# First products on tokens that are not normed yet: factor and shift applied to the sums

## The chip, the cores and the metric

The kernel runs on one core of one Trainium2 chip. The metric is the device time of one execution in microseconds (us), from three runs of the kernel.

## The reference, cut to what matters

A layer of a diffusion trunk over 384 tokens (128 context tokens and 256 latent tokens), width 2048. The adaLN modulation gives a scale and a shift for each feature and kind of token; the tokens are normed, modulated and multiplied by one large projection:

```
mod = silu(c) @ w_ada + b_ada                      # six parts of 2048
h = rmsnorm(x, norm_mix) * (1.0 + sc1) + sh1       # x: 384 x 2048
z = h @ w_in                                       # w_in: 2048 x 5632, eleven groups of 512 columns
```

Four token mixers work on the groups of `z`; an output projection, a second modulated norm and a gated MLP follow (`w_out`, `w_up`, `w_down`).

## The kernel before

Features lie on the partitions. The 2048 features are 16 row tiles of 128, and a token tile `x[i]` holds four of them (128 x 4 x 384). Every float32 product is made of three matmuls on rounded halves: high by high, high by low, low by high (`mm_a`, `mm_b`). The weights come as chunks of 128 x 1024; ScalarE casts a chunk to its high half `whi`, VectorE subtracts for the low half `wlo`.

The projection `w_in` runs in three rounds over the row tiles: tiles 0 and 1, tiles 2 to 5, tiles 6 to 15 (`ROUNDS`). In each round all eleven groups (V, GBV, U, DX, CC, CH, CB and four heads H0 to H3) take their part, and their sums are kept in SBUF as `z`, first copied by ScalarE (`ev_first`), then added by VectorE (`ev_add`). Between the chunks of a round stand chunks of `w_ada`, so that scale and shift of the next row tiles are there in time. Most of these are matmuls of few columns on PE (`ada_pe`); the tile `START_DVE` is summed by VectorE (`ada_dve`, the tile `aacc`) and brought into columns by matmuls (`ps_mod`, L502).

At the start, `input_squares`, `input_pairs`, `input_sums` and `input_norm` compute the norm of all tokens: ScalarE squares, VectorE adds pairs, PE sums over the partitions (`ps_n`, L428), ScalarE takes the root, VectorE the reciprocal `bc1`. Then `split_affine` makes row tile 0: times `bc1` on VectorE, scale and shift on ScalarE, cast to `hh`, low half `hl`. The first chunks (`win_duo`) hold two groups of one row tile each: V with GBV, U with DX. `keep_warm` issues matmuls whose result nobody reads.

The order of the instructions on every engine is written by a planner (`Pipe`), which books an estimated cost for each instruction on a clock per engine. DMAs are issued on SP's queue in the order of the chunks; chunks marked `early` come first. Work outside the main stream (low halves, norms, evacuations that are more than one instruction) runs in threads; a thread that doesn't split weights is held back while the booked backlog of VectorE or ScalarE is over 2.5 us. All large tiles come from one pool of 20 slots.

The helpers for VectorE and ScalarE record every operation under L90, so the profile tells them apart by their tiles.

Of the kernel before, what the change touches and what calls it, by code (L numbers as in the profile page):

```python
# [14 lines left out]
P = 128  # L15
D = 2048
# [20 lines left out]

ROUNDS = ((0, 2), (2, 6), (6, 16))
# [8 lines left out]
WARM = (6, 8)  # L47
# [9 lines left out]
T_DMA = 1.46  # L57
TABLES = (AF.Silu, AF.Sigmoid, AF.Gelu_apprx_tanh, AF.Exp, AF.Sqrt)
# [35 lines left out]
class Pipe:  # L94
# [5 lines left out]
    def __init__(self, nc, pools, look_dma, look_split, backlog):  # L100
        self.nc = nc
        self.V = Engine(nc.vector, self, "d", 0.075, 1.04e-3, 0.52e-3, ("tensor_copy", "tensor_scalar"))
        self.S = Engine(nc.scalar, self, "a", 0.1, 0.83e-3, 0.83e-3, ())
        self.pools = pools
        self.LD, self.LS = look_dma, look_split
        self.backlog = backlog
        self.chunks = []
        self.threads = []
        self.now = 0.0
        self.clock = {"d": 0.0, "a": 0.0, "q": 12.0}  # L110
        self.end = 0.0
# [44 lines left out]
    hold = True  # L156
# [38 lines left out]
    def run(self):  # L195
        n = len(self.chunks)
        nxt, ahead, loaded = 0, 0, 0
        for c in sorted((c for c in self.chunks if "early" in c), key=lambda c: c["early"]):
            self.dma(c)
        for i in range(-1, n):  # L200
# [4 lines left out]
            while loaded < n:  # L205
                if "early" in self.chunks[loaded] or self.chunks[loaded].get("spare") is not None:
                    loaded += 1
                    continue
# [26 lines left out]
def trunk(ctx, tc, a, o):  # L235
# [28 lines left out]
    def slot(name, dtype=F32, shape=(P, 4, T)):  # L264
        return sp.tile(list(shape), dtype, tag="s", name=name)
# [141 lines left out]
    n1 = {}  # L407

    def input_squares(i):
        add_pos(x[i], i, pos, posr)  # L410
        n1[i] = slot("sq0")
        for k in range(0, 4, 2):
            S.activation(n1[i][:, k:k + 2], x[i][:, k:k + 2], AF.Square)
# [6 lines left out]

    def input_pairs(i):
        V.tensor_add(n1[i][:, 0:2], n1[i][:, 0:2], n1[i][:, 2:4])

    def input_sums(i):
        if i == 0:
            n1["ps"] = misc("ps_n1")
        for k in range(2):
            PE.matmul(n1["ps"][:, 0:T], ones, n1[i][:, k], start=i == 0 and k == 0, stop=i == 3 and k == 1)  # L428

    def input_norm():  # L430
        v1 = row_tile("v1")
        S.activation(v1, n1["ps"][:, 0:T], AF.Sqrt, bias=eps, scale=1.0 / D)
        V.reciprocal(bc1, v1)
# [111 lines left out]

    h_done, h_queue, h_workers = set(), [], []

    def h_worker():
        while h_queue:
            yield from h_make(h_queue.pop(0))  # L550
        h_workers.pop()

    def h_make(j):
# [3 lines left out]
        if j == 0:  # L557
            yield next(parts)
            pipe.hold = False
            pipe.finish(pipe.splits[0])  # L560
# [29 lines left out]
    def win_duo(i, k):  # L590
        def mm(c):
            need_h(k + 1)
            for n, grp in enumerate(DUOS[i]):
                n_acc, width = win_shape(grp)
                if k == 0:
                    z[grp] = slot(f"z{grp}", shape=(P, n_acc, width))
                for m in range(n_acc):
                    t = acc("acc0")
                    s = slice(512 * n, 512 * n + 512)
                    yield win_product(grp, t, m, k, c["hi"][:, s], c["lo"][:, s], True, True)  # L600
                    (ev_add if k else ev_first)(z[grp], m, t[:, 0:width])
        return dict(src=a["w_in_1"][i, k], mm=mm)

    def win_group(grp, rnd, evac):
# [4 lines left out]
        for k0 in range(k_lo, k_hi, 2):  # L609
            def pre(k0=k0):  # L610
                if rnd < 2 or grp == 0:
                    need_h(k0 + 2)
                if rnd == 2 and k0 == k_lo:
# [7 lines left out]
            def mm(c, k0=k0):  # L621
                if k0 == k_lo:
                    accs.extend(acc(f"acc{m}") for m in range(n_acc))
                    if rnd == 0:
                        z[grp] = slot(f"z{grp}", shape=(P, n_acc, width))
                hi = c["hi"].rearrange("p (k n) -> p k n", k=2)
                lo = c["lo"].rearrange("p (k n) -> p k n", k=2)
                for m in range(n_acc):
                    for kk in range(2):
                        yield win_product(grp, accs[m], m, k0 + kk, hi[:, kk], lo[:, kk], k0 + kk == k_lo, k0 + kk == k_hi - 1)  # L630
                    if k0 + 2 == k_hi:
# [267 lines left out]
    def rounds(rnd, evac):  # L899
# [3 lines left out]
        out.insert(1, win_duo(0, 1))  # L903
        out.insert(3, win_duo(1, 1))
        return out

    def make_h(js):
        h_queue.extend(js)
        for _ in range(min(2 - len(h_workers), len(js))):
# [3 lines left out]
    def ada_first(j):  # L913

        place = [(0, j, 1), (1, j, 1)]
        return [dict(ada_pe(a["w_ada_0"][j, k4], (0, -j), 4 * k4, 4, place, lambda: make_h((j,))), spare=-1) for k4 in range(4)]
# [16 lines left out]
    for rnd, (k0, k1) in enumerate(ROUNDS):  # L933
        ada = [c for j2s in START[rnd] for cs in zip(*[two_by_two(j2) for j2 in j2s]) for b in cs for c in b]
        if rnd == 0:
            t0, t1, d0, d1 = ada_first(0), ada_first(1), win_duo(0, 0), win_duo(1, 0)
            for i, c in enumerate(t0 + [d0, t1[0], d1] + t1[1:]):
                c["early"] = i
            side = t0 + [d0] + t1 + [d1]
# [261 lines left out]
    for i in range(4):  # L1201
        input_squares(i)
        if i:
            input_pairs(i - 1)
            input_sums(i - 1)
    input_pairs(3)
    input_sums(3)
    input_norm()
    pipe.chunks[4]["pre"] = lambda: (keep_warm(WARM[1]), need_h(1))
# [119 lines left out]
```

## Time and profile before

| | us |
|---|---|
| runs | 1779.76, 1780.69, 1780.70 |
| median | 1780.69 |
| the profiled execution | 1778.78 |
| its span, first to last instruction | 1777.0 |

| engine | busy us | share of the span |
|---|---|---|
| PE (TensorE, matmuls) | 1743.4 | 98% |
| DVE (VectorE) | 1113.9 | 63% |
| ACT (ScalarE) | 699.9 | 39% |
| POOL (GpSimd) | 20.4 | 1% |

Matmuls are pipelined, so a busy PE need not be PE at its peak: the distance from start to start tells more. An idle engine costs nothing unless another one waits for it; the profile names for each wait what ended it.

### The profile page before, as it was taken

What the parts mean: (1) busy time and instruction counts of PE and PEld (TensorE: products, weight loads), DVE (VectorE), ACT (ScalarE), POOL (GpSimd) and SP (SyncE); (2) the same over time, 40 slices, a digit from 0 to 9 for tenths busy, and PEclk for the clock granted to TensorE, in tenths of its full rate; (3) what the DMA queues carried; (4) which work ended last, traced back from release to release, by engine and by line L of the source; (5) the groups of instructions that cost most, each with busy time, mean ns of one, the idle gap of its engine ahead of it and who ended that gap; (6) DMA issues with size and microseconds to landing.
All of it is one profiled execution on the core that took longest, in us unless ns stands there. A gap on an engine that the chain in (4) does not pass through costs nothing.

```text
span 1777.0 us, 27701 instructions
## 1 busy us (share of the span) xinstructions
PE 1743.4 (98%) x11244; PEld 1680.6 (95%) x11244; DVE 1113.9 (63%) x1911; ACT 699.9 (39%) x1044; POOL 20.4 (1%) x35
## 2 busy tenths in 40 slices
PE   8999999999999999999999999999999999999996
PEld 6989889999989989999999999999999999999996
DVE  4595678888986577899884344465453345545444
ACT  5523333234743256343342223344332234434331
POOL 0000000000001000000000000000000000000000
PEclk9999999999999999999999999999999999999998
DMA  8878776576645855656654444434444444444431
GB/s 335 285 281 307 283 250 229 182 251 213 221 132 181 289 212 158 196 184 206 210 177 136 127 123 130 128 117 135 130 121 130 130 122 129 129 124 127 131 119 72
DMA packets 89664, 317.29 MB, mean 179 GB/s; under 512 B 9856, under 2 KB 14208, under 8 KB 89536
## 3 DMA queue, kind: packets, MB, share of 16 engines
q1 hardware_dynamic: 87520, 308.58, 53.5%
q0 software_dynamic: 1728, 6.55, 1.1%
q8 instruction: 88, 1.44, 0.3%
q10 hardware_dynamic: 288, 0.39, 0.1%
q14 instruction: 40, 0.33, 0.1%
HBM read 311.82 MB, written 3.67 MB: 178 GB/s over the span
## 4 chain that ended last, share of the span: by engine, by line
issue 63%; PE 7%; DVE 1%; DMA 0%; POOL 0%; ACT 0%; POOLq 0%; DVEq 0%
PE acc L520 2%; PE acc L521 2%; PE acc L522 2%; DVE xr L90 1%; DMA xr<-in_xT 0%; PE ps_sc L286 0%; PE ps_bc L286 0%; PE ps_ada L464 0%; PE ps_o L286 0%; DVE wlo L90 0%; DVE sqacc L90 0%; POOL hg_q L381 0%; PE ps_ms L286 0%; DVE hw L90 0%; ACT kq L90 0%
## 5 line engine op out<-in xcount | busy, mean ns | idle before, releaser
L90 DVE TENSOR_TENSOR wlo<-raw,whi 128x1024 fp32r<-128x1024 f32 x384 | 469.2, 1222 | 490.8 <-ACT whi L90 488.5
L90 ACT CAST whi<-raw 128x1024 fp32r<-128x1024 f32 x384 | 402.7, 1050 | 878.2 <-PE acc L521 646.0
L520 PE MATMUL acc<-h2h,whi 128*128 128x384 f32 x1408 | 470.9, 334 | 0.2 <-ACT h2h L90 0.2
L521 PE MATMUL acc<-h2l,whi 128*128 128x384 f32 x1408 | 470.5, 334 | 0.3
L522 PE MATMUL acc<-h2h,wlo 128*128 128x384 f32 x1408 | 470.3, 334 | 0.0
L520 PEld LDWEIGHTS acc<-h2h,whi 128*128 128x128 f32 x1408 | 264.3, 188 | 1.8 <-ACT h2h L90 1.0
L521 PEld LDWEIGHTS acc<-h2l,whi 128*128 128x128 f32 x1408 | 264.3, 188 | 0.8 <-DVE h2l L90 0.8
L522 PEld LDWEIGHTS acc<-h2h,wlo 128*128 128x128 f32 x1408 | 264.3, 188 | 0.0
L522 PE MATMUL acc<-gh,wlo 128*128 128x384 f32 x704 | 235.1, 334 | 0.0
L520 PE MATMUL acc<-gh,whi 128*128 128x384 f32 x704 | 235.1, 334 | 0.0
L521 PE MATMUL acc<-gl,whi 128*128 128x384 f32 x704 | 235.1, 334 | 0.0
L520 PE MATMUL acc<-hh,whi 128*128 128x384 f32 x576 | 199.2, 346 | 0.9 <-DVE z L90 0.9
L522 PE MATMUL acc<-hh,wlo 128*128 128x384 f32 x576 | 193.3, 336 | 0.5 <-DVE wlo L90 0.4
L521 PE MATMUL acc<-hl,whi 128*128 128x384 f32 x576 | 192.8, 335 | 0.1
L90 DVE SCALAR_TENSOR_TENSOR aacc<-raw,svp,aacc 128x512 f32<-128x512 f32 x270 | 184.8, 745 | 0.0
L90 DVE SCALAR_TENSOR_TENSOR glu<-up,sm,glu 128x127 f32<-128x127 f32 (+1 forms) x352 | 135.3, 415 | 30.4 <-ACT glu L90 24.2
L520 PEld LDWEIGHTS acc<-gh,whi 128*128 128x128 f32 x704 | 132.1, 188 | 0.0
L521 PEld LDWEIGHTS acc<-gl,whi 128*128 128x128 f32 x704 | 132.1, 188 | 0.0
L522 PEld LDWEIGHTS acc<-gh,wlo 128*128 128x128 f32 x704 | 132.1, 188 | 0.0
L520 PEld LDWEIGHTS acc<-hh,whi 128*128 128x128 f32 x576 | 108.1, 188 | 11.8 <-issue 7.1
L521 PEld LDWEIGHTS acc<-hl,whi 128*128 128x128 f32 x576 | 108.2, 188 | 1.0 <-DVE hl L90 0.4
L522 PEld LDWEIGHTS acc<-hh,wlo 128*128 128x128 f32 x576 | 108.1, 188 | 1.1 <-DVE wlo L90 1.1
(154 smaller groups left out, 1540.3 us busy)
## 6 DMA issues: line engine op xcount, KB each, us to landing
raw<-in_w_up SPq DMA_DIRECT2D x176, 512.0 KB, 3.6
raw<-in_w_in SPq DMA_DIRECT2D x88, 512.0 KB, 4.7
raw<-in_w_down SPq DMA_DIRECT2D x88, 512.0 KB, 3.5
raw<-in_w_ada SPq DMA_DIRECT2D x64, 512.0 KB, 5.7
raw<-in_w_ada_dve SPq DMA_DIRECT2D x64, 512.0 KB, 4.5
raw<-in_w_ada_pe SPq DMA_DIRECT2D x64, 512.0 KB, 5.4
raw<-in_w_out SPq DMA_DIRECT2D x32, 512.0 KB, 4.3
x<-in_xT SPq DMA_DIRECT2D x4, 768.0 KB, 7.8
```

The costliest lines, as they stand in the source:

```text
L90: return f(*args, **kw)
L520: PE.matmul(out, wh, xh, start=first, stop=False)
L521: PE.matmul(out, wh, xl, start=False, stop=False)
L522: PE.matmul(out, wl, xh, start=False, stop=last)
```

## The change

Six groups of the first round (U, DX, CC, CH, CB, H0) no longer wait for the norm. Since the norm is a factor per token, `W (A x r + B) = r (W A x) + W B`: their matmuls take `uh`, `ul`, the high and low half of `A x` for tokens not yet normed, with the shift `B` as two further columns (386 columns in place of 384). When the norm is known, `fix` multiplies the kept sums by `bc1`, 24 multiplications of 128 x 384 on VectorE, and the evacuation in the second round adds the shift, per range of tokens, from the two extra columns (`ev_shift`). V, GBV and H1 to H3 work on normed tokens as before, later in the round.

So the loads of `x[1]` to `x[3]` move behind the first CC chunk, the norm becomes threads that run beside the products (squares added up by VectorE in `sqacc`, three small matmuls, a power on GpSimd, diagonal matrices, three matmuls to spread the rows), and the order of the chunks changes: U at row tile 0, the adaLN of row tile 1, DX, CC, CH, CB, H0, V with GBV twice, U with DX at row tile 1, H1 to H3. Every slot is 1568 elements long, so that all of them begin on multiples of 128 bytes though six tiles have rows of 386.

```diff
+PLAIN = (W_U, W_DX, W_CC, W_CH, W_CB, W_H0)
-WARM = (6, 8)
+WARM = (6, 3)
+AHEAD = (0.0, 3.0, 1.0)
+X_THERE = (5.0, 21.0, 23.5, 26.0)
+SLOT = 1568
...
     def run_threads(self):
         for th in list(self.threads):
             own = th[0] in self.splits
-            if own and self.hold:
-                continue
...
         for c in sorted((c for c in self.chunks if "early" in c), key=lambda c: c["early"]):
+            if c["early"] in self.between:
+                self.between[c["early"]]()
+                self.clock["q"] += 3 * T_X
             self.dma(c)
...
-    load_x(1, x[1], SY)
-    load_x(2, x[2], SY)
-    load_x(3, x[3], SY)
+    pipe.between = {len_early: lambda: [load_x(i, x[i], SY) for i in range(1, 4)] for len_early in (10,)}
...
+    def input_norm():
+        while len(squared) < 4:
+            yield 0.3
+        yield "d"
+        ps = misc("ps_n1")
+        mean_square_rows(ps, sqacc)
+        yield 0.3
+        q = rstd_of(ps, NG, D, "n1")
+        yield 0.9
+        dgs = diags(q)
+        yield
+        bc = misc("ps_bc1")
+        broadcast_rows(bc, dgs)
+        yield 0.2
+        S.copy(bc1, bc[:, 0:T])
...
+    def plain_make(j):
+        if not plain:
+            plain.extend(slot(n, F32R, (P, 2, 400)) for n in ("uh", "ul"))
+        uh, ul = plain[0][:, j, 0:T + 2], plain[1][:, j, 0:T + 2]
+        A, B, src = mods[:, 1, j], mods[:, 0, j], x[0][:, j]
+        for t0, t1, v in RANGES:
+            S.activation(uh[:, t0:t1], src[:, t0:t1], AF.Copy, scale=A[:, v:v + 1])
+        S.copy(uh[:, T:T + 2], B)
+        yield "a"
+        for t0, t1, v in RANGES:
+            V.scalar_tensor_tensor(out=ul[:, t0:t1], in0=src[:, t0:t1], scalar=A[:, v:v + 1], in1=uh[:, t0:t1].bitcast(F32), op0=ALU.mult, op1=ALU.subtract)
+        V.tensor_sub(ul[:, T:T + 2], B, uh[:, T:T + 2].bitcast(F32))
...
+    def plain_slot(grp):
+        t = slot(f"z{grp}", shape=(P, 4, T + 2))
+        return t[:, :, 0:T], t
...
+    def fix(grp):
+        i = PLAIN.index(grp)
+        while grp not in summed or i and PLAIN[i - 1] not in fixed:
+            yield 0.3
+        for m in range(4):
+            zt = z[grp][:, m]
+            V.tensor_mul(zt, zt, bc1)
+            yield 1.2
+        fixed.add(grp)
+
+    def ev_shift(grp, zt, m, t):
+        for t0, t1, v in RANGES:
+            V.scalar_tensor_tensor(out=zt[:, m, t0:t1], in0=t[:, t0:t1], scalar=wb[grp][:, m, T + v:T + v + 1], in1=zt[:, m, t0:t1], op0=ALU.add, op1=ALU.add)
...
+                if rnd == 1 and grp in PLAIN and k0 == k_lo:
+                    pipe.finish(fixes[grp])
...
+                    elif k0 + 2 == k_hi and rnd == 1 and grp in PLAIN:
+                        ev_shift(grp, z[grp], m, accs[m])
...
-        out.insert(1, win_duo(0, 1))
-        out.insert(3, win_duo(1, 1))
+        out[len(PLAIN) - 2:len(PLAIN) - 2] = [win_duo(0, 0), win_duo(0, 1), win_duo(1, 1)]
...
-            side = merge_streams(main, ada, count(ada) / (len(main) - 1.0))
+            if rnd == 1:
+                for i in range(2):
+                    main[i]["early"] = 9 + i
+            side = merge_streams(main, ada, count(ada) / (len(main) - AHEAD[rnd]))
...
-    pipe.chunks[4]["pre"] = lambda: (keep_warm(WARM[1]), need_h(1))
+    pipe.chunks[4]["pre"] = lambda: keep_warm(WARM[1])
```

## Rows read from the trace of the kernel before

**Rows 1.** The page's first part: busy us, share of the span, instructions of each engine.
```profile
PE 1743.4 (98%) x11244; PEld 1680.6 (95%) x11244; DVE 1113.9 (63%) x1911; ACT 699.9 (39%) x1044; POOL 20.4 (1%) x35
```

**Rows 2.** Windows by stage: stretch, length, busy us (instructions) per engine, granted clock, DMA.
```profile
25.98:84.60 58.62, 58.47 (x637) 52.30 (x638) 28.36 (x47) 34.86 (x64) 0.00 (x0) 1.00 0.86 304
84.60:132.00 47.40, 45.51 (x349) 39.66 (x348) 41.62 (x67) 12.69 (x16) 0.00 (x0) 1.00 0.75 266
```

**Rows 3.** Timeline of the start: start us, us, engine, line, instruction [idle before, releaser].
```profile
12.86 7.27 PE L428 MATMUL ps_n<-sq,misc_c 128*128 128x384 f32 x16 [3.01 <-DVE sq L90]
...
20.64 1.04 ACT L90 CAST whi<-raw 128x1024 fp32r<-128x1024 f32 x1
...
24.40 0.98 ACT L90 ACTIVATE ht<-ht,mods 128x128 f32<-128x128 f32 x2 [2.72 <-DVE ht L90]
...
25.98 0.50 PE L525 MATMUL acc<-whi,hh 128*128 128x512 f32 x1 [0.28 <-ACT hh L90]
```

**Rows 4.** Windows of the first 30 us; the last number is GB/s.
```profile
0.00:10.00 10.00, 5.21 (x12) 3.88 (x12) 2.22 (x7) 2.66 (x3) 0.53 (x8) 1.00 0.82 274
10.00:30.00 20.00, 16.86 (x177) 11.57 (x178) 12.31 (x23) 12.02 (x20) 0.00 (x0) 0.91 1.04 405
```

**Rows 5.** DMA issues of the first 60 us: count, size of one, median us to landing.
```profile
raw<-in_w_ada SPq DMA_DIRECT2D x23, 512.0 KB, 10.2
...
x<-in_xT SPq DMA_DIRECT2D x4, 768.0 KB, 7.8
pos<-in_pos_c ACTq DMA_DIRECT2D x1, 256.0 KB, 5.4
sm<-in_smalls SPq DMA_DIRECT2D x1, 236.0 KB, 5.5
```

**Rows 6.** PE timeline, first round: a 24-product chunk starts, an adaLN pair, the next chunk.
```profile
53.22 0.44 PE L520 MATMUL acc<-hh,whi 128*128 128x384 f32 x1
...
57.60 1.08 PE L464 MATMUL ps_ada<-raw,svp 128*32 128x128 f32 x32
58.61 0.44 PE L520 MATMUL acc<-hh,whi 128*128 128x384 f32 x1
```

**Rows 7.** PE timeline where the second round begins.
```profile
84.47 0.39 PE L525 MATMUL acc<-whi,hh 128*128 128x512 f32 x1
84.70 0.40 PE L526 MATMUL acc<-wlo,hh 128*128 128x512 f32 x1
```

**Rows 8.** Instructions on the tile `ps_bc`, a later norm's broadcast: ns min/median/max, first and last start.
```profile
L286 PE MATMUL ps_bc<-dg,misc_c x36: 271/275/579, 507.2 to 1763.5; 128*128 128x128 f32 x36
```

**Rows 9.** VectorE by line and shape, first 600 us: busy us, mean ns, idle before.
```profile
L90 DVE TENSOR_TENSOR z<-acc,z 128x384 f32<-128x384 f32 x80 | 42.0, 551 | 21.3 <-PE acc L522 21.0
...
L90 DVE TENSOR_TENSOR ht<-x,bc 128x384 f32<-128x384 f32 x16 | 8.3, 552 | 0.0
...
L90 DVE SCALAR_TENSOR_TENSOR xr<-acc,mods,xr 128x256 f32<-128x256 f32 x12 | 5.7, 475 | 0.0
...
L90 DVE SCALAR_TENSOR_TENSOR xr<-acc,mods,xr 128x128 f32<-128x128 f32 x12 | 4.2, 346 | 1.0 <-PE acc L522 0.9
```

**Rows 10.** VectorE timeline, 84.5 to 133 us: the two idle stretches in its busiest part.
```profile
104.76 1.22 DVE L90 TENSOR_TENSOR wlo<-raw,whi 128x1024 fp32r<-128x1024 f32 x1 [3.16 <-ACT whi L90]
...
114.96 1.23 DVE L90 TENSOR_TENSOR wlo<-raw,whi 128x1024 fp32r<-128x1024 f32 x1 [0.54 <-ACT whi L90]
```

**Rows 11.** PE timeline, 112 to 130 us: the three instructions that waited for VectorE.
```profile
113.54 0.44 PE L520 MATMUL acc<-hh,whi 128*128 128x384 f32 x1 [0.69 <-DVE z L90]
...
123.60 0.44 PE L520 MATMUL acc<-hh,whi 128*128 128x384 f32 x1 [0.22 <-DVE z L90]
...
128.21 1.00 PE L502 MATMUL ps_mod<-aacc,pick 128*32 128x128 f32 x16 [0.82 <-DVE aacc L90]
```

**Rows 12.** Windows around the stretch at the lower granted clock (column after POOL).
```profile
9.00:12.80 3.80, 0.85 (x3) 0.34 (x1) 2.38 (x6) 3.79 (x6) 0.00 (x0) 1.00 1.07 373
12.90:16.20 3.30, 3.30 (x5) 1.75 (x6) 3.30 (x9) 2.44 (x4) 0.00 (x0) 0.50 1.02 404
```

More of the change, by code (lines that the diff above doesn't have):

```diff
@@ L109, in __init__ @@
         self.now = 0.0
[L110 removed]
+        self.clock = {"d": 0.0, "a": 0.0, "q": T_FIRST}
         self.end = 0.0
@@ L205, in run @@
             while loaded < n:
-                if "early" in self.chunks[loaded] or self.chunks[loaded].get("spare") is not None:
+                if "early" in self.chunks[loaded] or "src" not in self.chunks[loaded] or self.chunks[loaded].get("spare") is not None:
                     loaded += 1
@@ L264, in slot @@
     def slot(name, dtype=F32, shape=(P, 4, T)):
-        return sp.tile(list(shape), dtype, tag="s", name=name)
+        t = sp.tile([P, SLOT], dtype, tag="s", name=name)
+        n = 1
+        for d in shape[1:]:
+            n *= d
+        return t[:, 0:n] if len(shape) == 2 else t[:, 0:n].rearrange("p (a b) -> p a b", b=shape[2])
     def row_tile(name):
@@ L419, in keep_warm @@
             PE.matmul(ps[:, 0:2 * P], ident, misc_c, start=True, stop=True)
[L421 to L433, printed above, removed]
     def columns(ps, n, place):
@@ L544, in h_slots, with need_plain, ev_plain @@
         hl[i] = slot(f"{name}l{i}", F32R)
+    plain, plain_done, wb = [], set(), {}
+    def plain_make(j):
[6 more added lines that the diff above has]
+        S.copy(uh[:, T:T + 2], B)
+        yield "a"
+        for t0, t1, v in RANGES:
+            V.scalar_tensor_tensor(out=ul[:, t0:t1], in0=src[:, t0:t1], scalar=A[:, v:v + 1], in1=uh[:, t0:t1].bitcast(F32), op0=ALU.mult, op1=ALU.subtract)
+        V.tensor_sub(ul[:, T:T + 2], B, uh[:, T:T + 2].bitcast(F32))
+        plain_done.add(j)
+    def need_plain(n):
+        while not all(k in plain_done for k in range(n)):
+            for th in list(pipe.threads):
+                if th in pipe.threads and th[0] not in pipe.splits + stats:
+                    pipe.step(th)
+    def plain_slot(grp):
+        t = slot(f"z{grp}", shape=(P, 4, T + 2))
+        return t[:, :, 0:T], t
+    def ev_plain(grp, zt, m, t, add):
+        if add:
+            V.tensor_add(wb[grp][:, m], t[:, 0:T + 2], wb[grp][:, m])
+        else:
+            S.copy(wb[grp][:, m], t[:, 0:T + 2])
+        if m == 3 and (add or grp not in sum(DUOS, ())):
+            summed.add(grp)
+    def fix(grp):
[10 more added lines that the diff above has]
+            V.scalar_tensor_tensor(out=zt[:, m, t0:t1], in0=t[:, t0:t1], scalar=wb[grp][:, m, T + v:T + v + 1], in1=zt[:, m, t0:t1], op0=ALU.add, op1=ALU.add)
     h_done, h_queue, h_workers = set(), [], []
@@ L549, in h_worker @@
         while h_queue:
+            while not normed:
+                yield 0.3
             yield from h_make(h_queue.pop(0))
@@ L915, in ada_first @@
         place = [(0, j, 1), (1, j, 1)]
-        return [dict(ada_pe(a["w_ada_0"][j, k4], (0, -j), 4 * k4, 4, place, lambda: make_h((j,))), spare=-1) for k4 in range(4)]
+        return [dict(ada_pe(a["w_ada_0"][j, k4], (0, -j), 4 * k4, 4, place, lambda: pipe.start(plain_make(j))), spare=-1) for k4 in range(4)]
     def ada_start(j2):
@@ L1200, in trunk @@
     keep_warm(WARM[0])
[L1201 to L1208, printed above, removed]
-    pipe.chunks[4]["pre"] = lambda: (keep_warm(WARM[1]), need_h(1))
+    add_pos(x[0], 0, pos, posr)
+    for i in range(5):
+        stats.append(input_squares(i) if i < 4 else input_norm())
+        pipe.spawn(stats[i], X_THERE[i] if i < 4 else 0.0)
+    pipe.chunks[4]["pre"] = lambda: keep_warm(WARM[1])
     pipe.run()
```

90 lines of the change are left out of this document (69 added, 21 removed).

## The prediction

> **What bounds the kernel now.** I read the page's busy table first: TensorE (PE) is busy 98% of the span [rows 1]. So a change can gain only where PE has no useful work, and lose where it makes PE wait. The windows by stage show where that is: from 25.98 to 84.60 us PE is busy 58.47 of 58.62, from 84.60 to 132 it loses 1.9 us [rows 2]. Before 25.98 it has no projection to do at all, and the timeline of the start says why [rows 3]. PE sums the squares of the four token tiles until about 20, ScalarE and VectorE turn them into the norm factor, the first normed row tile is made, and the first product of `w_in` follows at 25.98, released by that tile's cast on ScalarE (`hh`). So 26 us at the start are the prize. What limits how soon products can start without the norm is the DMA: 274 GB/s in the first 10 us, 405 from 10 to 30 [rows 4].
>
> **The change, part by part.**
>
> *The start.* A raw weight tile is 512 KB (0.524 MB), a token tile 768 KB (0.786 MB), the small tables 256 and 236 KB [rows 5], with two more of 128 x 256 and 128 x 32 numbers 0.65 MB. Two bursts matter.
>
> First product: it needs one token tile, the tables, four `w_ada_0` tiles and the pair U+DX: 0.79 + 0.65 + 5 x 0.524 = 4.06 MB. By [rows 4] 2.74 MB have moved at 10 us and the rest takes 1.32/0.405 = 3.3 us, so 13.3. From last byte to use I add 0.7, an estimate between 0 and the 1.5 us that lie between 6.42 MB (19.1 by the same sum) and the cast of the first pair at 20.64 [rows 3]. Then ScalarE casts the pair (1.04), scales the two ranges of row tile 0 (0.98 for two such ranges) and copies two columns (about 0.2): 16.2. VectorE still has the low half of the pair (1.22 [rows 10]) and that of the row tile: about 17.1. From there PE runs U (12 products, half of the 4.38 us of a 24-product chunk [rows 6]), the second `w_ada_0` tile (last byte about 19.2, done about 21), DX, and with row tile 1 (about 24) the chunk CC, done about 27.9.
>
> Second burst: CC is followed by the adaLN pair and CH. The first 13 raw tiles, four token tiles and tables are 6.82 + 3.15 + 0.65 = 10.6 MB, moved at 10 + 7.88/0.405 = 29.4; with 0.7 more the second of the pair is usable at 30.1, and CH starts at 30.9. PE waits here, so some 1.5 to 2.5 us of anything late before it cost nothing; if that cover is used up, each us late is a us lost.
>
> *From there to the end of the first round* the products are those of before: seven chunks of 24 products (CH, CB, H0, U+DX of the second row tile, H1, H2, H3) of 4.38, two of V+GBV at 18 x 0.23 + 0.2 = 4.34, seven adaLN pairs of 1.01 [rows 6, 7]: 30.7 + 8.7 + 7.1 = 46.4. Added: the norm on PE inside the stream, six matmuls for the sums, six for the broadcast, at 0.275 each [rows 8]; alone 3.2, overlapped perhaps 0.6, I take 1.3, as they sit among other matmuls. The two extra columns: 144 products x 2/384 x 0.18 = 0.1. Round two then begins at 30.9 + 46.4 + 1.4 = 78.7 instead of 84.47 [rows 7]: **5.8 us gained**. Own bounds 4.0 (norm at its full price) to 6.7. The norm's chain itself (tiles 1 to 3 landing by about 26.5, adds, power, diagonals) ends near 39; V+GBV, the first to need it, comes at about 48, so it lies beside 9 us of other work.
>
> *VectorE in the second round.* Added on it: 24 multiplications by the factor (`fix`), of the form 0.552; in the evacuation of six groups one add of 0.551 becomes two scaled adds out of PSUM, by the nearest rows 0.475 + 0.346, so +0.27 each, 24 times, or +0.19 after the 0.08 overlap of neighbours [rows 9]. Total some 11 + 5 us. Removed at the start: a reciprocal. In most of the kernel VectorE has room, but not from 88 to 132 us, where it computes an adaLN tile itself: in the VectorE timeline of that stage I find only 3.16 and 0.54 us idle [rows 10], and PE waited there for it: 0.69 and 0.22 for a group's old sums, 0.82 for the adaLN accumulators [rows 11]. Queued behind an added instruction are the low halves of weights, the evacuations and these accumulations. How many multiplications fall there is decided by the planner (threads wait while its booked backlog exceeds 2.5 us; a `fix` waits 1.2 us after each). `fix` starts when the second U chunk is summed, about 65; at one per 2 us or so eight are out before 78.7. In the stage itself the planner's own booked load fills VectorE, so I expect about one in 4 us: three or four ahead of the 3.16 idle, which hides them, three after it. Behind it: 3 x 0.47 + 8 evacuations x 0.19 = 2.9, less the 0.54 idle, = 2.4 of lag for PE to wait out. Against it, the 0.82 wait is for matmuls that the planner places by its booked clock, which now counts the added work, so they move behind PE work and that wait can vanish; part of the lag also lands after PE's last need. I take a loss of **1.0**, bounds -1.7 (all three waits gone) and 3.0.
>
> *Nothing else.* H0, CB and the rest get evacuated at the same place by the same ScalarE copy; plain casts of two row tiles cost ScalarE and VectorE some 4 us at the start, where both idle. SLOT only lays tiles out: no row shows a row start that costs, so 0; its bad case is a rival. SP's queue: the three token tiles move behind CC; everything behind them (CH, the pair) is in the second burst's sum.
>
> **Sum.** The profiled execution took 1778.78 (span 1777.0); 1778.78 - 5.8 + 1.0 = 1774.0. The median of the runs shown, 1780.69, lies 1.9 above that execution, so I forecast 1780.69 - 4.8 = **1775.9**; its own range, a gain of 7.2 to 2 (the ends of both terms hardly coincide), is 1773.5 to 1778.7.
>
> **Rivals.**
> *B, VectorE takes half of it back:* lag not absorbed, 2.5 to 5 us lost; net gain about 2, 1778.5. For it: idle of 0.54 in 27 us, and weight buffers are freed by VectorE, so lag also delays transfers. Against: the planner holds threads back when its backlog is high.
> *C, the clock:* the granted clock fell to 0.50 (1.2 GHz) in 12.9 to 16.2, after 3.8 us in which PE was busy 0.85 [rows 12]. In the changed kernel PE is busy in pieces from 10 to 17 and waits for the pair near 29. If U, the adaLN tile and DX run at half clock they take some 6 us more (2.1 + 2 + 2.1), CC ends at 34 instead of 27.9, and beyond the cover some 3.8 of the 5.8 are gone: 1779.7. The Trainium skill ("TensorE: Matmul & The Clock Gate", section on HAM oscillation) says that matmuls after a long enough wait for DMA start cold; by it this would be the forecast. The row agrees for a wait of 3 us; but over 10 to 30 us the mean granted was 0.91 [rows 4], so the level came back soon, and the waits I expect are shorter.
> *D, slower:* all 24 multiplications come ahead of the adaLN tile's last accumulation, because the planner books short. 24 x 0.47 + 12 x 0.19 = 13.6, less 3.7 idle, = 9.9 lost against 5.8: +4.1, 1784.8. It beats the gain from about 16 of them in that stretch. For it: finish() forces a group's four just ahead of its second round. Against: only U, DX and CC come due by then.
> *E, the width or the layout costs:* 144 products of 386 columns at the 0.23 of 512 columns instead of 0.18 [rows 6, 7], or rows that start off a round address: 144 x 0.05 = 7.2, so 1783.1. Nothing in the trace shows a width that falls off a step.
> *F, it doesn't do what it says:* the norm comes late and V+GBV waits for it, or row tile 0 isn't ready early. Nine us of cover speak against; it would end near 1780.
>
> **How the numbers follow.** About 0.2% (3.6 us) is what a measurement of this kernel can tell from no change. Forecast 0.60, of which 0.50 gains over 3.6 and 0.10 less; B 0.18, C 0.08 and F 0.02 all within 0.2%, less 0.03 of them faster; D 0.08 and E 0.04 slower, of which half of E stays within 0.2%. So faster 0.53, same 0.37, slower 0.10. The range leaves out D, E, and the best of the forecast: 1773.5 to 1781.0.
>
> **What would show it.** Right: the first `w_in` product at 16 to 17.5 us; CH's products at about 31, waited for by DMA; round two (the 512-column products in a row) at 78 to 79.5; multiplications in VectorE spread from 65 on, under eight between the 3.16 idle's place and the last accumulation; PE's waits for VectorE there between 0 and 4 us in sum. Wrong: PE waits between 31 and 79, a clock of 0.50 after 20 us, first products later than 20, or a steady distance between products above 0.18.

## The result: 0.66% slower, and the profile after

The changed kernel took 1792.35 us (median of 4 runs, 1791.02 to 1794.26), the kernel before 1780.70 beside it (1779.76 to 1781.34): 1.0066 times as long, 95% interval 1.0053 to 1.0078. The prediction was 1775.9, with a range up to 1781.0; the time lies 11 us above that range. The profiled execution took 1791.02 and its span is 1789.0, where before it was 1778.78 and 1777.0: 12.0 more.

The first thing to look at is not the stage that was changed. These are the page's first part and the costliest PE groups, first after, then before (busy us and mean ns of one behind the bar):

```profile
PE 1754.5 (98%) x11230; PEld 1692.9 (95%) x11230; DVE 1131.8 (63%) x1975; ACT 699.0 (39%) x1050; POOL 22.1 (1%) x36
...
L549 PE MATMUL acc<-h2h,whi 128*128 128x384 f32 x1408 | 475.0, 337 | 0.2 <-ACT h2h L98 0.2
L550 PE MATMUL acc<-h2l,whi 128*128 128x384 f32 x1408 | 473.7, 336 | 0.3 <-DVE h2l L98 0.2
L551 PE MATMUL acc<-h2h,wlo 128*128 128x384 f32 x1408 | 473.0, 336 | 0.0
```

```profile
L520 PE MATMUL acc<-h2h,whi 128*128 128x384 f32 x1408 | 470.9, 334 | 0.2 <-ACT h2h L90 0.2
L521 PE MATMUL acc<-h2l,whi 128*128 128x384 f32 x1408 | 470.5, 334 | 0.3
L522 PE MATMUL acc<-h2h,wlo 128*128 128x384 f32 x1408 | 470.3, 334 | 0.0
```

PE is busy 11 us longer than in [rows 1] with 14 instructions fewer, and what grew is the MLP, whose code the change does not touch. In its up projection, shown here, the same 1408 products per line are each 2 to 3 ns longer; its down projection grew in the same way. The next view shows it without a model of where a matmul ends. It is the same 500 us in the MLP, in which PE never waits, first of the kernel before, then after; the number in brackets behind PE's busy time counts its matmuls:

```profile
1100.00:1600.00 500.00, 500.00 (x2887) 500.00 (x2886) 244.72 (x376) 190.61 (x254) 0.00 (x0) 1.00 0.42 127
```

```profile
1100.00:1600.00 500.00, 500.00 (x2856) 500.00 (x2855) 247.57 (x384) 189.65 (x256) 0.00 (x0) 1.00 0.41 126
```

31 products fewer in 500 us at the full granted clock: 500/2887 = 173.2 ns from one to the next before, 500/2856 = 175.1 after. That is 1.1%, on an engine that is busy 98% of the span.

So the account by stage, from the starts of the same products in both traces, is:

```
                                        before     after    difference
first projection product                 25.98     15.56
second round begins                      84.47     80.98      -3.5
  from there to product 768             117.08    117.93      +0.85
  from product 768 to the last product 1555.79   1571.15     +15.4
  last product to the end of the span    19.6      19.0       -0.7
span                                    1777.0    1789.0     +12.0
```

Product n is the n-th of the 9120 matmuls into the accumulators, counted from 0; product 768 is the 13th of the third round, behind the stage in which VectorE computes an adaLN tile itself. The gain at the start was real, though 2.3 us short of the 5.8 predicted. VectorE's stage cost 0.85 where 1.0 was predicted. What decided is the 15.4 us behind it, a term that the prediction set to 0.

The start itself went much as described. PE timeline after, first projection products (start us, us, engine, line, instruction, idle before and its releaser), then the windows of 2 to 3 us there, with the granted clock in the column after POOL:

```profile
15.56 0.44 PE L549 MATMUL acc<-uh,whi 128*128 128x386 f32 x1 [0.99 <-ACT uh L98]
16.76 0.44 PE L550 MATMUL acc<-ul,whi 128*128 128x386 f32 x1 [0.76 <-DVE ul L98]
...
17.57 0.48 PE L551 MATMUL acc<-uh,wlo 128*128 128x386 f32 x1
17.85 0.53 PE L549 MATMUL acc<-uh,whi 128*128 128x386 f32 x1
18.17 0.52 PE L550 MATMUL acc<-ul,whi 128*128 128x386 f32 x1
```

```profile
15.56:17.50 1.94, 1.18 (x5) 0.92 (x6) 1.15 (x4) 0.08 (x1) 0.00 (x0) 1.00 1.02 408
17.50:20.00 2.50, 2.50 (x13) 2.06 (x15) 0.00 (x0) 1.37 (x3) 0.00 (x0) 0.52 1.02 396
20.00:22.40 2.40, 2.40 (x129) 2.31 (x129) 0.00 (x0) 0.48 (x1) 0.00 (x0) 0.78 1.06 373
```

The first product starts at 15.56 (predicted 16.2), the second at 16.76 (17.1). Then, after PE had idled 0.99 and 0.76 us before them, the granted clock falls to 0.52: products start 0.32 us apart instead of 0.17.

### The profile page after: what moved, and what is told of

Read it like the earlier page. It is cut to its first block, busy times and chain, and to the rows that moved or that the text cites. A ratio compares the mean times of both kernels' runs of the same rounds, so it can differ in the third digit from the quotient of the medians.

```text
span 1789.0 us, 27778 instructions
## 1 busy us (share of the span) xinstructions
PE 1754.5 (98%) x11230; PEld 1692.9 (95%) x11230; DVE 1131.8 (63%) x1975; ACT 699.0 (39%) x1050; POOL 22.1 (1%) x36
## 4 chain that ended last, share of the span: by engine, by line
issue 63%; PE 7%; DVE 1%; DMA 0%; POOL 0%; ACT 0%; POOLq 0%; DVEq 0%
PE acc L549 2%; PE acc L551 2%; PE acc L550 2%; DVE xr L98 1%; DMA xr<-in_xT 0%; PE ps_sc L298 0%; PE ps_ada L493 0%; PE ps_bc L298 0%; PE ps_o L298 0%; DVE wlo L98 0%; DVE sqacc L98 0%; POOL hg_q L391 0%; PE ps_ms L298 0%; DVE hw L98 0%; ACT kq L98 0%
## 5 line engine op out<-in xcount | busy, mean ns | idle before, releaser
L549 PE MATMUL acc<-hh,whi 128*128 128x384 f32 x528 | 183.9, 348 | 2.3 <-DVE z L98 2.2
L551 PE MATMUL acc<-hh,wlo 128*128 128x384 f32 x528 | 178.0, 337 | 0.4 <-DVE wlo L98 0.3
L550 PE MATMUL acc<-hl,whi 128*128 128x384 f32 x528 | 177.4, 336 | 0.0
L549 PEld LDWEIGHTS acc<-hh,whi 128*128 128x128 f32 x528 | 99.1, 188 | 12.3 <-issue 9.4
L551 PEld LDWEIGHTS acc<-hh,wlo 128*128 128x128 f32 x528 | 99.1, 188 | 1.1 <-DVE wlo L98 1.1
L550 PEld LDWEIGHTS acc<-hl,whi 128*128 128x128 f32 x528 | 99.2, 188 | 0.6
```

Of the source, the lines that this page charges most:

```text
L549: PE.matmul(out, wh, xh, start=first, stop=False)
L550: PE.matmul(out, wh, xl, start=False, stop=False)
L551: PE.matmul(out, wl, xh, start=False, stop=last)
```

## What the runs tell apart

Two things had to be explained: the 15.4 us, and the 2.3 us missing at the start. For the first the theory was the slots. The change gives every slot 1568 elements, 6272 bytes, where it was 6144. In the built programs the weights' tiles (`whi`, `wlo`) begin 64 bytes past a multiple of 256 in both. Before, 6144 is 24 times 256, so in each of the 8832 products of 384 columns the moving row also begins 64 past such a multiple. After, 6272 is 24.5 times 256, and every other slot lies 128 bytes out of step with the weights (in step: as far past a multiple of 256 as they are); 4048 of the 8688 products of 384 columns read such a row. (So the slots do not begin on multiples of 128 bytes, as the section on the change has it, but 64 past them.) Within the changed kernel the distance from a product to the next, averaged by where its moving row begins (640 to 1760 us, starts of the trace against the addresses of the built program), is:

```
row begins, bytes past a multiple of 512      64     320     192     448
products                                    1614    1971    1213    1487
mean distance to the next, ns              172.9   173.7   177.7   177.7
```

The rival was that the new order of the work disturbs the products.

(The times of products in the expectations are 0.24 us later than in the profile's views, as they count from another zero. e1 to e12 are the labels of the runs; there is no e8.)

**e1, the layout alone.** The kernel before, with the slots of the change and nothing else:

```
+SLOT = 1568
...
-        return sp.tile(list(shape), dtype, tag="s", name=name)
+        t = sp.tile([P, SLOT], dtype, tag="s", name=name)
+        n = 1
+        for d in shape[1:]:
+            n *= d
+        return t[:, 0:n] if len(shape) == 2 else t[:, 0:n].rearrange("p (a b) -> p a b", b=shape[2])
```

> The kernel before with nothing of the change but the slots: each is a tile of 1568 elements a partition of which 1536 are used. Its SBUF addresses then are those of the changed kernel in kind: of the 8844 products with 384 columns, 3864 read a moving row that begins 192 bytes past a multiple of 256, the others 64 past one; before, all 8844 began 64 past a multiple of 512. Theory (where a row begins is what costs): in the changed kernel the distance to the next product averages 172.9 to 173.7 ns behind rows at 64 and 177.7 behind rows at 192, so 3864 x 4.4 ns = 17 us; 1780.7 + 17 = 1797.7, and products of the MLP stage 175 to 176 ns apart instead of 173.3. Rival (the new order of the work, not the layout, disturbs the products): within 0.2% of the kernel before, 1777 to 1784, products 173.3 ns apart.

Measured: 1793.74 us against 1781.18, ratio 1.0071 (1.0056 to 1.0086). The same window of this run:

```profile
1100.00:1600.00 500.00, 500.00 (x2864) 500.00 (x2863) 249.69 (x391) 192.18 (x261) 0.00 (x0) 1.00 0.42 126
```

174.6 ns a product. The tile size by itself makes the kernel before as slow as the changed one; the price was 12.6 us, not 17 (4.4 ns held for the changed kernel's sequence of rows, and e12 shows that the sequence matters). In its trace the stretch behind product 768 is 12.9 us longer than before; the changed kernel lost 15.4 there, with 175.1 ns a product. The stretch from product 252 to 768, with no work added to VectorE, took 118.06 us here, 0.98 more than before: the layout alone costs as much there as the changed kernel lost, 0.85.

**e2, the change without the layout.** The changed kernel with slots of 1536 elements; the two shift columns go to a small tile of their own:

```
-SLOT = 1568
+SLOT = 1536
...
-        t = slot(f"z{grp}", shape=(P, 4, T + 2))
-        return t[:, :, 0:T], t
+        return slot(f"z{grp}"), shifts[:, PLAIN.index(grp)]
...
-        if add:
-            V.tensor_add(wb[grp][:, m], t[:, 0:T + 2], wb[grp][:, m])
-        else:
-            S.copy(wb[grp][:, m], t[:, 0:T + 2])
+        for to, s in ((zt[:, m], t[:, 0:T]), (wb[grp][:, m], t[:, T:T + 2])):
+            if add:
+                V.tensor_add(to, s, to)
+            else:
+                S.copy(to, s)
...
```

> The changed kernel with slots of 1536 elements as before: the two extra columns of the six groups are evacuated into a small tile of their own, with an instruction of their own (24 small copies on ScalarE, 8 small adds on VectorE), and a 64-byte filler keeps every moving row 64 bytes past a multiple of 256. Theory (row starts): products are 173.3 ns apart again, the 2.0 ns that each of some 8700 had more go (17 us), the earlier second round stays (3.5 us): 1792.4 - 17 = 1775.4, within 1774 to 1778. Rival (the order of the work): the small copies change nothing, so it stays at 1790 to 1794 with products at 175.3.

Measured: 1778.97 (ratio 0.9989, 0.9980 to 0.9998), and

```profile
1100.00:1600.00 500.00, 500.00 (x2886) 500.00 (x2885) 244.13 (x376) 190.63 (x254) 0.00 (x0) 1.00 0.43 128
```

The distance is back at 173.3 with the new order of the work in place: the rival falls. The time is a microsecond above the range given: from product 252 to 768 this run took 118.78 us, 1.7 more than before, which is the matter of e5 and e11.

**e3, all rows and weights 64 bytes lower.** As e2 without the 64-byte filler, so that rows and weights begin on multiples of 256 bytes.

> As the run with 1536-element slots, without the filler: now every moving row begins on a multiple of 256 bytes exactly, and the weights' columns too. Theory (what costs is the start 192 past a multiple of 256, or another start than that of the row read before): no different from the run with rows at 64, 1775 to 1778, products 173.3 apart. Rival (each start has its own price): another distance between products; a gain or loss of 2 ns in each is 17 us, so outside 1770 to 1781.

Measured: 1777.22 (0.9975, 0.9965 to 0.9985), 2887 products in the same 500 us. The start as such has no price for the products; rows and weights in step have none at 0 either. (1.8 us less than e2 is within what the two intervals leave open.)

For transfers the start did matter. PE waits for them in the first 32 us, and e3 moved more there than e2; the window from 10 to 30 us, e2 and then e3, the last number being GB/s:

```profile
10.00:30.00 20.00, 17.36 (x311) 14.47 (x310) 9.65 (x28) 10.48 (x31) 0.00 (x0) 0.91 1.04 397
```

```profile
10.00:30.00 20.00, 16.86 (x286) 14.00 (x279) 9.75 (x28) 10.61 (x32) 0.00 (x0) 0.91 1.04 412
```

Weight tiles of 512 KB that follow one another land 1.28 us apart (median of the first 45 us) in each of the five traces whose weight tiles begin 64 bytes past a multiple of 256 (before, changed, e1, e2, e9), and 1.24 to 1.25 apart in each of the six in which they begin on one (e3, e5, e6, e7, e10, e11). So e3 and what is built on it have faster loads at the start than the changed kernel, which e10 comes back to.

**e9, the cost doubled.** The kernel before, with 128 bytes put between the weights' tiles and the slots:

```
+    gap = ctx.enter_context(tc.tile_pool(name="gap", bufs=1))
+    gap.tile([P, 32], F32, name="gap")
     sp = ctx.enter_context(tc.tile_pool(name="sp", bufs=20))
```

> The kernel before, with a filler of 128 bytes between the weights' tiles and the slots and nothing else: every one of the 8832 products of 384 columns now reads a moving row that begins 192 bytes past a multiple of 256 while its weights begin 64 past one. Theory (it costs where the moving row begins against the weights' columns: e4 gave 175.9 ns at this distance, 173.3 at none): 8832 x 2.5 = 22 us, and about 1 more for the 288 products of 512 columns (232 for 227 in e4): 1804, within 1800 to 1807, more than in the changed kernel, where half of the rows lie so. Rival (only a kernel that mixes two starts pays, as rows read one after the other differ): within 0.2% of the kernel before.

Measured: 1801.24 (1.0112, 1.0095 to 1.0129), 20.4 us more than before, and

```profile
1100.00:1600.00 500.00, 500.00 (x2843) 500.00 (x2842) 243.97 (x382) 191.12 (x259) 0.00 (x0) 1.00 0.41 125
```

175.9 ns a product: no instruction added, none moved, every row of these products now begins in the same place as every other, and the kernel is slower than the changed one, where not quite half of the rows lie so. With e1, e2 and e3 this settles the cause of the loss: where the slots lie against the weights, modulo 256 bytes.

**e4, the price by itself.**

> Nothing but products, 36 in a row for each of 50 pairs of starts (the moving row and the weights' columns in steps of 32 bytes through 512, some mixes, some with 512 columns); it leaves out the whole computation. Theory (a start 192 past a multiple of 256 is dear by itself): series whose rows all begin at 192 or 448 show 177 to 178 ns, those at 64 and 320 show 173.3, the weights' start shows nothing. Rival (only a change of start from one row to the next costs): every series with one start shows 173.3, and the series that mix 64 and 192 show 175 to 176.

Each series (54 were run; a part of them), mean distance of its products:

```
rows begin, weights begin (bytes past a multiple of 512)     ns
64, 64   0, 0   128, 128   192, 192   320, 64   64, 320      173.3 to 174.2
128, 64   384, 64   64, 0   64, 256                          173.2 to 173.3
0, 64   256, 64   64, 128   64, 384                          174.7
192, 64   448, 64   64, 192   64, 448                        175.9
rows 64 and 192 in turn, weights 64                          174.9
32, 64   96, 64   64, 96   64, 352                           173.3
160, 64   416, 64   64, 32   64, 160   64, 416               176.6 to 176.8
4, 64                                                        180.0
512 columns: 64, 64 / 192, 64 / 64, 192                      226.8 / 232.1 / 232.5
```

The theory's figure was wrong and its rule too narrow: 192 with 192 is as cheap as 64 with 64, so it is not a start that is dear but a distance; the rival's "every series with one start shows 173.3" is wrong as well. Among multiples of 64 only the distance between row and weights modulo 256 shows: 0 or 64 on is free, 64 back costs 1.4 ns, 128 costs 2.5. For multiples of 32 that rule breaks (rows at 96 with weights at 64 take 173.3, rows at 64 with weights at 32 take 176.6, the same distance), and with 512 columns the order of the prices is another: 64 on takes 228.9, 64 back 233.3, more than 128. No series lies by more than 0.2 under the 173.3 of the kernel before, so the products had nothing to gain from another layout.

**e12, whose weights?** While PE streams a row it loads the weights of the next product (PEld is busy 95% of the span). So a row might collide with its own weights or with the next ones.

> Nothing but products again (the whole computation is left out), 72 in a row for each of ten pairs of starts, all ten twice. It asks which weights a moving row must agree with: its own, or those that PE loads for the next product meanwhile. Series in which rows and weights alternate together (row 64 with its own weights 64, then 192 with 192) have own weights in step and the next product's 128 bytes off; series in which they alternate crosswise (64 with 192, then 192 with 64) have own weights off and the next product's in step. Theory (the row's reads meet the reads of the next product's weights): together 175.5 to 176, crosswise 173.3 to 174. Rival (what counts is a product's own weights): together 173.3 to 174, crosswise 175.5 to 176. Where only rows or only weights alternate, half of the products are off by either account: 174.5 to 175.

Windows of the first four series, 72 products each: in step (64, 64), out of step (192, 64), alternating together, alternating crosswise:

```profile
27.11:39.62 12.51, 12.51 (x74) 12.51 (x73) 0.00 (x0) 0.00 (x0) 0.00 (x0) 1.00 0.00 1
39.62:52.30 12.68, 12.68 (x74) 12.68 (x73) 0.00 (x0) 0.00 (x0) 0.00 (x0) 1.00 0.00 1
52.30:64.92 12.62, 12.62 (x74) 12.62 (x73) 0.00 (x0) 0.00 (x0) 0.00 (x0) 1.00 0.00 0
64.92:77.64 12.72, 12.72 (x74) 12.72 (x73) 0.00 (x0) 0.00 (x0) 0.00 (x0) 1.00 0.01 1
```

173.8, 176.1, 175.3 and 176.7 ns a product; the repeats agree to 0.3. Both accounts fall: together should have been as cheap as the first by one of them, crosswise by the other. Of these series only those in which all rows and all weights are in step are cheap. Which two reads meet is left open. The Trainium skill ("TensorE: Matmul & The Clock Gate", section "Step-by-step: what each phase is for") says that PE reads moving data and weights through two independent ports, so that loading the next weights takes nothing from the running matmul. These runs differ from it by up to 1.7% (12.51 to 12.72 us, with nothing changed but addresses and no other engine at work).

**e10, the clock at the start.** As e3, with more filler matmuls so that PE does not idle before the first product:

```
-WARM = (6, 3)
+WARM = (6, 7)
```

> As e3, with seven filler matmuls instead of three ahead of the first projection product, so that PE is busy through the 1.2 us before the first product and most of the 1.0 us in which the second waits for its low half. In e3 the granted clock was 0.59 from 17.5 to 20 us and the first twelve products took 6.8 us to the next ones, in e5 it was 1.00 and they took 5.3; CH began at 32.7 there and at 31.3 in e5. Theory (the half clock behind that gap holds up CC, and ScalarE's evacuation of CC ahead of the cast of CH): granted clock 1.00 from 17.5 to 22.5, CH at 31.3, second round 1.4 us earlier, 1775.8. Rival (bytes ahead of the adaLN pair set CH whatever the clock does): full clock, but CH at 32 to 33 and 1777. Second rival: the drop does not come from the gap; the clock falls all the same.

The window from 17.5 to 20, of e3 and then of e10, and in e10 the adaLN pair's second half, CH's first product and that of the second round:

```profile
17.50:20.00 2.50, 2.50 (x36) 2.06 (x37) 0.00 (x0) 1.92 (x8) 0.00 (x0) 0.59 1.02 404
```

```profile
17.50:20.00 2.50, 2.50 (x113) 2.25 (x115) 0.00 (x0) 1.66 (x8) 0.00 (x0) 1.00 1.03 407
```

```profile
30.38 0.64 PE L494 MATMUL ps_ada<-raw,svp 128*32 128x128 f32 x16 [0.56 <-DMA raw<-in_w_ada]
30.95 0.45 PE L677 MATMUL acc<-uh,whi 128*128 128x386 f32 x1
...
79.71 0.39 PE L555 MATMUL acc<-whi,hh 128*128 128x512 f32 x1
```

The clock stays at 1.00, CH begins at 30.95 after a wait for DMA, and the second round at 79.71 instead of 81.19 in e3. How a slow U reaches CH is seen in e3, PE and ScalarE:

```profile
28.82 0.48 ACT L98 COPY z<-acc 128x384 f32<-128x384 f32 x1 [2.19 <-PE acc L745]
...
29.78 1.31 PE L494 MATMUL ps_ada<-raw,svp 128*32 128x128 f32 x32
...
31.25 1.12 ACT L98 CAST whi<-raw 128x1024 fp32r<-128x1024 f32 x1
...
32.42 0.45 PE L677 MATMUL acc<-uh,whi 128*128 128x386 f32 x1 [1.32 <-ACT whi L98]
```

The cast of CH's weights stands on ScalarE behind the evacuation of CC, which waits for PE; CC ended late because U ran at half speed. Late work before the DMA wait was not free, as it passed through ScalarE's queue.

In the changed kernel two causes meet at CH:

```profile
31.13 1.08 ACT L98 CAST whi<-raw 128x1024 fp32r<-128x1024 f32 x1
...
31.74 0.64 PE L493 MATMUL ps_ada<-raw,svp 128*32 128x128 f32 x16 [0.54 <-DMA raw<-in_w_ada]
...
32.31 0.19 PEld L676 LDWEIGHTS acc<-uh,whi 128*128 128x128 f32 x1 [0.20 <-ACT whi L98]
32.31 0.45 PE L676 MATMUL acc<-uh,whi 128*128 128x386 f32 x1
```

The cast ends at 32.2, about as in e3 (32.4). But the second tile of the adaLN pair lands only at 31.69 here (30.41 in e3, 30.34 in e10), and CH follows that half of the pair by 0.57 us, as it does in e10. So the transfer alone would have put CH where it began, and full clock alone would have gained next to nothing there.

What the filler does to the clock is not quite settled either. From 17.5 to 20 us the granted clock was 0.50 to 0.59 in five traces without it (changed, e2, e3, e6, e7) and 1.00 in the two with it (e10, e11); but in e5, which has no filler and at the start the code of e3, it was 1.00 as well. So the drop does not come in each execution. By its median e10, 1776.76 (0.9972, 0.9962 to 0.9983), can't be told from e3.

**e7, the bytes ahead of the pair.**

```
-            if c["early"] in self.between:
-                self.between[c["early"]]()
-                self.clock["q"] += 3 * T_X
             self.dma(c)
...
                 self.dma(self.chunks[loaded])
+                behind += 1
+                if behind == 2:
+                    self.between[10]()
+                    self.clock["q"] += 3 * T_X
...
-X_THERE = (5.0, 21.0, 23.5, 26.0)
+X_THERE = (5.0, 26.0, 28.5, 31.0)
```

> As e3, with the three later token tiles (2.36 MB) issued behind CH and the first adaLN pair, not ahead of them. Theory (the bytes queued ahead of that pair set the start of CH, at 32.7 where 30.9 was predicted): the pair and CH follow CC without a wait for DMA, CH at 30.0 to 30.7; as the same bytes still come before CB and the norm, CB (38.6) hardly moves, and the second round begins at 80.5 to 82. Rival (the clock at half speed from 15 to 20 us sets it, or ScalarE): CH stays at 32 to 33. A second rival: the norm comes 5 us later and V+GBV waits for it, second round at 83 or later.

Measured: 1780.72 (0.9999, 0.9989 to 1.0008). CH starts at 30.67, without a wait for DMA, as the theory said. But the next chunk pays, and more than the same bytes: its first product, and PE's window behind it,

```profile
39.22 0.69 PE L678 MATMUL acc<-uh,whi 128*128 128x386 f32 x1 [3.03 <-ACT whi L98]
```

```profile
39.20:44.40 5.20, 5.18 (x16) 5.19 (x17) 4.05 (x6) 0.70 (x1) 0.00 (x0) 0.50 0.91 372
```

CB waits 3 us for its cast, whose tile lands late (38.14), the granted clock falls to 0.50 behind that wait, and the second round begins at 86.59, later than in the kernel before. I had expected 80.5 to 82. So the order of the change (tokens first) is the better one, and a wait of 3 us on PE costs its own length and then 5.2 us at half speed, in which half as many products run.

**e5, the multiplications left out.**

```
         for m in range(4):
-            V.tensor_mul(zt, zt, bc1)
-            yield 1.2
+            yield 0.1
```

> The changed kernel with 1536-element slots and rows on multiples of 256 bytes (the run e3), and the 24 multiplications of plain sums by the norm factor left out, so six groups stay unnormed. In e3 the second round begins at 81.4 and the second-round products of 384 columns lose ground in VectorE's own adaLN stage: from product 264 to product 768 it takes 116.6 us, 114.3 in the kernel before. Theory (VectorE's added work is what costs there, the multiplications most of it: eight of them at 0.47 from 84 to 130 us): the stretch comes back to 114 to 115 and the time to 1775 to 1776. Rival (the two scaled adds that replace one add, or the order of VectorE's queue alone): the stretch stays at 116 and the time at 1777.

Measured: 1775.83 (0.9973, 0.9961 to 0.9985); from product 264 to 768 it takes 114.97, from 252 to 768 117.73. That looks like the theory. But e10, which has all 24 multiplications, takes 114.95 and 117.71, and e3, with the same work in the same order, 116.58 and 119.34. So the multiplications are not shown to cost anything: with them the same work in the same order varies by 1.6 us here. (This run also kept the clock at 1.00 from 17.5 to 20, without any change there, and began its second round at 79.79.)

**e11, the multiplications earlier.**

```
+            elif normed and s.shape[-1] == T:
+                V.tensor_mul(to, s, bc1)
+                fixed.add((grp, m))
             else:
                 S.copy(to, s)
...
-            V.tensor_mul(zt, zt, bc1)
-            yield 1.2
+            if (grp, m) not in fixed:
+                V.tensor_mul(zt, zt, bc1)
+                yield 0.1
```

> As e10, with the multiplications earlier: H0's four by the norm factor in its evacuation, which comes after the norm (VectorE multiplies out of PSUM, ScalarE's copy goes), the others without the pause of 1.2 us that the planner put behind each. By the order on VectorE 18 of 24 come before the adaLN stage's sixth accumulation instead of 12. Theory (multiplications among the accumulations cost their 0.47 us each): from product 264 to product 768 it takes 115 to 116 us instead of 116.6, the time 1774.5 to 1775.5. Rival (the work crowds out the weights' low halves before 84 us): PE waits before product 264, and no gain against e10.

Measured: 1776.34 (0.9969, 0.9956 to 0.9981), from product 264 to 768 116.00 us: no shorter than e10's 114.95. Moving them ahead gains nothing that can be seen, so again no cost of theirs shows. e10 and e11 are the best versions here, both 0.3% under the kernel before; their intervals don't tell them apart.

**e6, the multiplications on GpSimd.**

```
-            V.tensor_mul(zt, zt, bc1)
+            G.tensor_mul(zt, zt, bc1)
```

> As e3, with the 24 multiplications issued on GpSimd, which is nearly idle, instead of VectorE. Theory (VectorE's load is what costs): the same as with the multiplications left out, 1775 to 1776. Rival (GpSimd is so slow with them, or so much in VectorE's way, that sums come late): VectorE's other instructions last longer than the 0.74 and 1.21 us of e3 beside them, or PE waits for a sum that GpSimd holds; 1777 to 1782.

Measured: 1781.70 (1.0005, 0.9996 to 1.0014): the rival. Instructions of VectorE from 82 to 130 us, first in e3, then in e6, and PE's waits in e6:

```profile
L98 DVE SCALAR_TENSOR_TENSOR aacc<-raw,svp,aacc 128x512 f32<-128x512 f32 x30 | 20.5, 739 | 0.0
L98 DVE TENSOR_TENSOR wlo<-raw,whi 128x1024 fp32r<-128x1024 f32 x9 | 10.9, 1214 | 5.2 <-ACT whi L98 5.2
```

```profile
L98 DVE SCALAR_TENSOR_TENSOR aacc<-raw,svp,aacc 128x512 f32<-128x512 f32 x28 | 21.4, 821 | 0.0
L98 DVE TENSOR_TENSOR wlo<-raw,whi 128x1024 fp32r<-128x1024 f32 x9 | 12.9, 1428 | 5.0 <-ACT whi L98 5.0
```

```profile
94.00 0.50 PE L555 MATMUL acc<-whi,hh 128*128 128x512 f32 x1 [1.96 <-DVE z L98]
116.21 0.66 PE L550 MATMUL acc<-hh,whi 128*128 128x384 f32 x1 [2.41 <-DVE z L98]
```

With GpSimd at work beside it VectorE's accumulations last 821 ns on average instead of 739 and the low halves 1428 instead of 1214, and PE waits 4.4 us for sums. The Trainium skill ("SBUF — State Buffer", section "Who interferes with whom") says that a VectorE instruction with two SBUF inputs contends with a GpSimd instruction that reads SBUF; these are such, and the rows agree.

## Why the prediction was wrong

By its steps:

- *"SLOT only lays tiles out: no row shows a row start that costs, so 0."* This is the step that failed, for 12.6 us by itself (e1) and 13.4 between the changed kernel and e2. No row of before could show a cost, since there every row began in step with the weights; that was no bound. The price was 1.4 ns a product on average in e1 and 1.9 in the changed kernel's MLP, and it was due on all that read a slot, some 8700, not on what was new. The rival for the layout named the right thing and counted 144 products for it at 50 ns; what came was 8700 at less than 2, so it expected 7 us in the first 80 and nothing later, and had a chance of 0.04. Its sign, "a steady distance above 0.18", was too coarse by far: 1% of this engine's time is 17 us, and 0.1751 passes below it.
- *The start, 5.8 gained:* 3.5 measured. First product 15.56: right. The norm's factor was there at 46.2, 7 us later than summed, and still 4 us ahead of the first product of V+GBV at 50.32; so PE did not wait for it, but half of the cover was gone. CH came 1.4 late. Its DMA term was short: the pair's second tile landed at 31.69, where 30.1 was summed, and only with tiles on multiples of 256 bytes (e10) did it come near, 30.34. Half clock from 17.5 ends at the same place: this was the clock rival, placed rightly (waits before U) but given 0.08 and priced at 3.8. Between e3 and e10, where the tile lands in time, it is 1.5, since the adaLN tile and DX were mostly through at full speed. "Anything late before it cost nothing" missed that CH's cast stands behind CC's evacuation on ScalarE. The rest, 0.9, lies between CH and the second round (48.67 us instead of 47.8): waits of 0.21 before CB and 0.26 for a low half of U and DX; what is left was not taken apart, and in the changed kernel the layout is in it.
- *VectorE, 1.0 lost (-1.7 to 3.0):* 0.85 measured. That the size came out is luck as far as the runs show: the layout alone costs 0.98 there (e1), the added work with rows in step 0.6 to 2.3 (e2, e3, e10, e11), so the two do not simply add up. The vanished wait for the adaLN accumulators did vanish, waits for sums came instead, 1.38 and 0.80 against 0.69 and 0.22 in [rows 11],

```profile
110.90 0.41 PE L549 MATMUL acc<-hh,whi 128*128 128x384 f32 x1 [1.38 <-DVE z L98]
...
121.54 0.41 PE L549 MATMUL acc<-hh,whi 128*128 128x384 f32 x1 [0.80 <-DVE z L98]
```

  but leaving the multiplications out or moving them changed nothing beyond the spread. The idle stretch of VectorE in [rows 10], 3.16 for a cast whose tile comes late, is still there, 2.52 long,

```profile
101.37 1.23 DVE L98 TENSOR_TENSOR wlo<-raw,whi 128x1024 fp32r<-128x1024 f32 x1 [2.52 <-ACT whi L98]
```

  and takes the earlier ones in, as the prediction had it. What makes the stretch vary by 1.6 us with the same code (e3, e10) is open; the arrival of that tile differs between them (VectorE idles 3.91 and 2.38), but e11 has 2.22 and is slow as well.
- *Signs.* Right: first product, PE's waits for VectorE (2.2 us in sum), the multiplications spread from 65 on, two of them (106.90 and 111.32) between the idle stretch and the last accumulation, where under eight were predicted. Wrong: CH at 32.31, round two at 80.98, and half clock earlier than "after 20 us" had it.

With rows in step the change lands inside the range, 1773.5 to 1781.0, but that does not bear out the whole sum. e2, which differs in the layout and 32 small instructions, took 1778.97: a gain of 2.2 us against its own kernel before, where 4.8 was summed. e3 and e10 gained 4.0 and 5.7, but their tiles also land faster, and e10 has the filler besides.

## What to carry to other kernels

A changed tile size moves every tile behind it, so its price is counted on all instructions that read any of them, and on an engine that is busy 98% of the span one nanosecond in each of 8700 products is 9 us. When such an engine's instruction time differs by a per cent between two kernels, sort the distances by the operands' addresses before looking at the order of the work; here slots whose size is a multiple of 256 bytes, as far from the weights as before, take the cost away. Two variants that differ in where their tiles begin can differ in their transfers as well, so the landings are compared before a gain is put down to something else. And a wait that will cover lateness has to be followed through the queues of the other engines, here ScalarE's, before the lateness is called free.

## What the runs showed that was not expected

- 384-column products go 173.3 to 174.2 ns apart where all moving rows and all weights begin in step modulo 256 bytes, 175.9 where they are 128 bytes apart; with 512 columns 226.8 and 232 (e4, e9).
- A single start is neither good nor bad: 64, 64, 0, 0 and 192, 192 are alike. A mix of starts costs even if each product's own pair, or each row and the next product's weights, are in step: 175.3 and 176.7 (e12).
- 512 KB weight tiles land 1.28 us apart where they begin 64 bytes past a multiple of 256 in SBUF, 1.24 where they begin on one (e2, e3 and nine other traces; no run was made for it alone).
- Behind a wait of PE of 3.0 us the granted clock was 0.50 over the next 5.2 us (e7); behind two of 0.99 and 0.76 us 0.52 over 2.5 us (the changed kernel), and with those filled by matmuls 1.00 (e10); in e5 it was 1.00 without the filling.
- 24 multiplications of 128 x 384 on GpSimd took 32.4 us, and VectorE's instructions beside them were 11 to 18% longer (e6).
